# Regrouping PSUM reads in a two-layer attention step: ScalarE copies first, VectorE differences behind them, and a later return of one bank

## The chip, the cores and the metric

The kernel runs on one core of a Trainium2 chip. The time is the device time of one execution in microseconds (us); of several runs the median is given. A core has five engines that run beside each other, each through its own instructions in order: TensorE (PE, matrix products into PSUM; its weight loads are shown apart as PEld), VectorE (DVE), ScalarE (ACT), GpSimd (POOL) and SyncE (SP, which here issues DMAs). PSUM has eight banks of 128 partitions by 512 fp32 numbers; SBUF holds everything else.

## The reference

One inference step of a trunk of two layers, for 512 latent tokens and 128 context tokens, with 1024 channels, 16 heads of 64, and a feed-forward width of 2816. All is fp32. Each layer is attention and then a gated convolutional feed-forward network (FFN), each between two RMS norms with a shift, scale and gate from a conditioning vector. Cut to what matters here:

```python
for l in range(2):
    hp, hs = modulated norms of the context xp and the latents xs
    if l == 0:                       # neighbourhood attention (NA)
        q, k, v = h @ na_w_qkv
        op  = blocked_attention(qp, kp, vp)
        os_ = neighbourhood_attention(qs, ks, vs, cache_k, cache_v, na_rpb)
    else:                            # grouped-query attention (GQA), 4 heads of keys
        q, k, v = h @ gqa_w_qkv      # q and k with an RMS norm per head, rotary positions on latents
        op  = blocked_attention(qp, kp, vp)
        os_ = softmax(qs k_all^T / 8) v_all      # 512 latent + 128 cached keys
    x = x + gate * rmsnorm(o @ w_o)
    x = x + gate * rmsnorm(conv_ffn(modulated norm of x))
```

The outputs are the two streams and the new keys and values of the context.

## The kernel before, in words

**Number format.** A product of two fp32 matrices is done as three products of parts: `hi` (the number rounded by a copy into a narrower matmul format, mostly on ScalarE) and `lo` (the number less `hi`, on VectorE or GpSimd): hi·hi, hi·lo, lo·hi. So each operand that comes out of a matmul is read twice from its PSUM bank, once by the copy and once by the difference, and the bank is free for TensorE's next use only after both. Weights are split in SBUF: `wh` from `wr` at L176 on ScalarE, `wl` at L178 on VectorE or GpSimd.

**What sets the order.** All TensorE instructions are chained in the order of the program (`pe()`). A scheduler orders the other engines; `behind(a, b)` (a dependency that only sets an order) puts `a` after `b` on their engine. `Banks` is a first-in first-out queue of PSUM banks: `get` takes the one returned longest ago, `put` returns one when the last read of it has been written down in the program, not when it has run. The taker then waits on the chip for those reads.

**Stages, with the profile's times.** NA with the projections of its queries, keys and values woven in, one item of work after another (`stream()`), up to about 300 us; its output projection (`m0`) to 330; the first FFN to 810; the GQA projections to 907; the GQA attention loop to 1037; its output projection (`m1`) to 1100; the second FFN to the end.

**Queries and keys in NA.** For each pair of heads (8 pairs) the projected queries sit in one bank `qk` one after the other in two halves of the columns: one piece of 256 columns, then one of 384 with a second piece of 64 (the shapes 64x256, 64x384 and 64x64 in the profile). Each of the two heads of a pair owns 64 partitions. For each piece and head, ScalarE writes the scaled query into `qs` (L957) and VectorE the low part (L958), in turn. For keys, `k_put` writes `kh` (L925, and for all pairs but the first a second copy into the other 64 partitions, L926) and `kl` (L927).

**End of NA.** The output projection needs the attention outputs as `oh`, `ol` (L1097) and four groups of weights; `OW` says at which part of the last projection item three of those are split. The group at part 7 has its difference on VectorE, the other two on GpSimd. `kp` (L973) is a copy of a key block that TensorE transposes into `tk`.

**End of the first FFN.** For a tile of tokens, `Finish` computes the norm and the next layer's modulated input `xm`, with scalars `ro` from GpSimd (L381) and the shift in L421; these feed `tr`, TensorE's transposes. At the same time the first weights of the GQA projection are split for the product `gp`.

**GQA attention.** 32 units: 8 head pairs, each with two heads and two halves of the queries. A unit has two score tiles `s`, for each of which VectorE finds the maximum (`nmg`, L1796), ScalarE the exponentials `gp` with their sum (L1799), VectorE the reciprocal (`rcg`, L1801) and GpSimd the multiplication (L1802); this is done two units ahead of the transposes. TensorE transposes a unit's `gp` in three groups of chunks (`turns(0)`, `(1)`, `(2)`, into `tp`), each copied to `pk` (ScalarE L1813 or VectorE L1815), and `values` multiplies them into `po`, a bank that collects both halves of a pair. Four banks serve the `tp`, `po` and the leftover transposes of queries `tq`. The steps of even and odd units are

```python
GORDER = ("s0 p v s1 t0".split(), "s0 l1 l2 t0 s1 t1 t2".split())
```

where `v` is `values` of the two units before, `t` are transposes of this unit, `l` of the unit before, and `p` one leftover piece of the projections. After the second half of a pair, `po` is split into `ph` (ScalarE, L1832) and `pl` (VectorE, L1833), and the context's columns of `ph`, `pl` are split from `opr` by GpSimd (L1840, L1841).

## Time and profile before

| | |
|---|---|
| median of 3 runs | 1544.62 us (1543.17 to 1544.98) |
| profiled execution, its own time | 1544.49 us |
| its span | 1542.7 us |
| granted TensorE clock, mean | 0.999 |
| busy: PE, PEld | 1510.3 us (98%), 1342.4 us (87%) |
| busy: DVE, ACT, POOL | 1013.9 us (66%), 854.0 us (55%), 701.1 us (45%) |

In rows of the trace, the first number is the start in us from the span's start, the second the length; then engine, line, operation, out<-in (names of tiles, numbers left out), the shape, and how many instructions the row groups. `[0.95 <-DVE rcg L1801]` says that the engine stood idle for 0.95 us before the row, and which instruction ended that by the profile. Where an instruction waits for several others, the one that came last is named. Ends of matmuls are modelled, so a row's end can overlap the next row's start.

### The profile page before, as it was taken

What the parts mean: (1) busy time and instruction counts of PE and PEld (TensorE: products, weight loads), DVE (VectorE), ACT (ScalarE), POOL (GpSimd) and SP (SyncE); (2) the same over time, 40 slices, a digit from 0 to 9 for tenths busy, and PEclk for the clock granted to TensorE, in tenths of its full rate; (3) what the DMA queues carried; (4) which work ended last, traced back from release to release, by engine and by line L of the source; (5) the groups of instructions that cost most, each with busy time, mean ns of one, the idle gap of its engine ahead of it and who ended that gap; (6) DMA issues with size and microseconds to landing.
All of it is one profiled execution on the core that took longest, in us unless ns stands there. A gap on an engine that the chain in (4) does not pass through costs nothing.

```text
span 1542.7 us, 26131 instructions
## 1 busy us (share of the span) xinstructions
PE 1510.3 (98%) x9710; PEld 1342.4 (87%) x9710; DVE 1013.9 (66%) x1653; ACT 854.0 (55%) x1628; POOL 701.1 (45%) x602
## 2 busy tenths in 40 slices
PE   7999999999999999999999999999999999999998
PEld 5999989779999999988887877778999999998886
DVE  5544343659776676764747777672988887885454
ACT  5665564655655555644544447762666665564343
POOL 1655554332355445533544454432335666553433
PEclk9999999999999999999999999999999999999999
DMA  9755444263675664487574420005533334459664
GB/s 350 190 153 127 125 136 105 61 212 103 195 226 188 206 204 141 138 290 263 187 223 137 123 83 28 1 20 195 169 114 108 117 110 156 128 162 302 196 219 134
DMA packets 196667, 243.99 MB, mean 158 GB/s; under 512 B 11484, under 2 KB 153020, under 8 KB 196540
## 3 DMA queue, kind: packets, MB, share of 16 engines
q1 hardware_dynamic: 186924, 235.85, 47.6%
q10 hardware_dynamic: 9616, 6.48, 2.5%
q8 instruction: 76, 1.25, 0.3%
q14 instruction: 51, 0.42, 0.1%
HBM read 214.38 MB, written 26.34 MB: 156 GB/s over the span
## 4 chain that ended last, share of the span: by engine, by line
PE 64%; DVE 7%; issue 2%; POOL 2%; ACT 1%; DMA 1%; ACTq 0%; DVEq 0%; POOLq 0%
PE acc L117 19%; PE ux L117 17%; PE uz L117 9%; PE uy L117 5%; PE gp L117 3%; PE y L117 2%; PE s L117 2%; PE po L117 2%; PE tp L120 2%; PE ada L117 1%; DVE B L250 1%; DVE nmg L1796 1%; DMA gn<-in_gqa_k_norm 1%; DMA wr<-in_ffn_w_up 1%; DVE wl L178 0%
## 5 line engine op out<-in xcount | busy, mean ns | idle before, releaser
L178 POOL TENSOR_TENSOR wl<-wr,wh 128x1024 fp32r<-128x1024 f32 x70 | 171.2, 2450 | 238.5 <-ACT wh L176 238.3
L117 PE MATMUL ux<-B,wh 128*128 128x322 f32 x832 | 200.5, 312 | 0.7 <-ACT u L1349 0.4
L1294 POOL TENSOR_TENSOR wl<-wr,wh 128x1024 fp32r<-128x1024 f32 x76 | 181.5, 2410 | 42.1 <-ACT wh L1293 38.3
L1373 DVE SCALAR_TENSOR_TENSOR t<-C,cw,t 128x644 f32<-128x644 f32 x176 | 156.3, 888 | 51.2 <-ACT t L1370 50.7
L117 PE MATMUL acc<-wh,alo 128*128 128x512 f32 x440 | 172.0, 391 | 0.0
L117 PE MATMUL acc<-wh,ahi 128*128 128x512 f32 x440 | 171.9, 391 | 0.0
L117 PE MATMUL acc<-wl,ahi 128*128 128x512 f32 x440 | 171.8, 390 | 0.0
L176 ACT CAST wh<-wr 128x1024 fp32r<-128x1024 f32 x138 | 143.5, 1047 | 37.8 <-DMA wr<-in_ffn_w_down 26.0
L117 PE MATMUL uz<-B,wh 128*128 128x322 f32 x640 | 155.9, 312 | 0.0
L117 PEld LDWEIGHTS ux<-B,wh 128*128 128x128 f32 x832 | 143.5, 189 | 4.2 <-ACT u L1349 1.4
L1262 DVE TENSOR_TENSOR alo<-ain,ahi 128x384 fp32r<-128x384 f32 (+1 forms) x88 | 70.5, 819 | 94.0 <-ACT ahi L1260 93.7
L117 PE MATMUL ux<-B,wl 128*128 128x322 f32 x416 | 129.3, 311 | 0.2 <-DVE wl L799 0.2
L117 PE MATMUL qk<-hT,wh 128*128 128x384 f32 (+1 forms) x512 | 122.4, 315 | 0.0
L117 PEld LDWEIGHTS uz<-B,wh 128*128 128x128 f32 x640 | 110.9, 189 | 2.9 <-issue 0.8
L1293 ACT CAST wh<-wr 128x1024 fp32r<-128x1024 f32 x84 | 85.0, 1049 | 47.1 <-DVE wr L1318 46.7
L1294 POOL TENSOR_TENSOR vl<-wr,vh 128x1024 fp32r<-128x1024 f32 x38 | 98.5, 2593 | 20.0 <-ACT vh L1293 19.7
L178 DVE TENSOR_TENSOR wl<-wr,wh 128x1024 fp32r<-128x1024 f32 x68 | 91.3, 1352 | 19.3 <-ACT wh L176 18.7
L1370 ACT ACTIVATE t<-C,cw 128x644 f32<-128x644 f32 x88 | 78.6, 893 | 44.0 <-DVE C L1401 31.6
L1260 ACT CAST ahi<-ain 128x384 fp32r<-128x384 f32 (+1 forms) x88 | 39.7, 460 | 108.9 <-PE acc L117 96.6
L117 PE MATMUL uz<-B,wl 128*128 128x322 f32 x320 | 99.5, 311 | 0.4 <-POOL wl L1294 0.3
L117 PEld LDWEIGHTS acc<-wh,alo 128*128 128x128 f32 x440 | 82.6, 188 | 17.8
L117 PEld LDWEIGHTS acc<-wh,ahi 128*128 128x128 f32 x440 | 82.6, 188 | 17.8
(264 smaller groups left out, 3893.6 us busy)
## 6 DMA issues: line engine op xcount, KB each, us to landing
wr<-in_ffn_w_up SPq DMA_DIRECT2D x88, 512.0 KB
wr<-in_ffn_w_down SPq DMA_DIRECT2D x88, 512.0 KB
wr<-in_ada_w SPq DMA_DIRECT2D x72, 512.0 KB
act<-act SPq DMA_DIRECT2D x44, 321.0 KB
wr<-in_na_w_qkv SPq DMA_DIRECT2D x24, 512.0 KB
mod<-modrow SPq DMA_DIRECT2D x20, 512.0 KB
ain<-act SPq DMA_DIRECT2D x44, 192.0 KB
wf<-in_ada_w SPq DMA_DIRECT2D x16, 512.0 KB
```

What stands on the lines that cost most here:

```text
L117: pe(nc.tensor.matmul(*a, **k))
L120: pe(nc.tensor.transpose(*a, **k))
L176: i = nc.scalar.copy(hi, raw)
L178: j = (low or nc.vector).tensor_sub(lo, raw, f32(hi))
L250: return nc.vector.tensor_sub(lo, src, f32(hi))
L1260: pin(nc.scalar.copy(hi[:, 0 : c1 - c0], ain[:, 0 : c1 - c0]))
L1262: i = nc.vector.tensor_sub(lo[:, 0 : c1 - c0], ain[:, 0 : c1 - c0], f32(hi[:, 0 : c1 - c0]))
L1293: nc.scalar.copy(hl[0], src)
L1294: return low.tensor_sub(hl[1], src, f32(hl[0]))
L1370: nc.scalar.activation(t, taps(0), AF.Identity, bias=cw[:, 3, n : n + 1], scale=cw[:, 1, n : n + 1])
L1373: nc.vector.scalar_tensor_tensor(t, taps(d), cw[:, w, n : n + 1], t, op0=ALU.mult, op1=ALU.add))
L1796: self.red[i] = nc.vector.tensor_reduce(nm, sv, axis=AX.XY, op=ALU.min)
```

## The change

Five edits.

1. In NA's `k_put` and query pieces, all ScalarE copies of one bank come first, then all VectorE instructions on it. The order-only dependencies that tied `oh`/`ol` of the first two pairs to those copies (`qput`, `splits`) are gone.
2. The third group of `m0`'s weights is split at part 4 of the last item instead of part 7, with its difference on VectorE as before.
3. The order-only dependency that put the first half of `xm`'s shift behind the first `wl` of the GQA projection (`fin.moved`, `lowered`) is gone.
4. In `turn_k` and `turn_q` both heads' ScalarE copies come first, then both differences (with the DMAs that spread the keys).
5. In `values`, `po`'s bank is no longer returned at once but at the end of the next odd unit (`ta["old"]`); `pl` is put behind the VectorE copy of `turns(1)` instead of behind a reduction; and GpSimd's split of the context's columns stays in program order instead of being put behind the last norm.

```diff
-OW = {0: 0, 2: 1, 7: 2}
+OW = {0: 0, 2: 1, 4: 2}
...
-            self.moved = [
+            return [
                 nc.vector.scalar_tensor_tensor(
...
-            ]
-            return self.moved[0]
+            ][0]
...
                     i = nc.scalar.copy(d["kh"][b][own, c0:c1], src[own])
-                    j = (nc.scalar.copy if p else nc.vector.tensor_copy)(d["kh"][b][oth, c0:c1], src[own])
-                    n = nc.vector.tensor_sub(d["kl"][b][own, c0:c1], src[own], f32(d["kh"][b][own, c0:c1]))
-                while splits and c0 == 0:
-                    for x, y in zip(splits.pop(), (j, n)):
-                        behind(x, y)
+                    if p:
+                        nc.scalar.copy(d["kh"][b][oth, c0:c1], src[own])
+                for b in range(2):
+                    own, oth = own_oth(b)
+                    if not p:
+                        nc.vector.tensor_copy(d["kh"][b][oth, c0:c1], src[own])
+                    nc.vector.tensor_sub(d["kl"][b][own, c0:c1], src[own], f32(d["kh"][b][own, c0:c1]))
...
                     for qc, pc in pieces:
                         for b in range(2):
                             own, oth = own_oth(b)
+                            nc.scalar.activation(d["qs"][b][own, qc], pp[own, pc], AF.Copy, scale=-0.125)
+                    for qc, pc in pieces:
+                        for b in range(2):
+                            own, oth = own_oth(b)
                             q = d["qs"][b]
-                            j = nc.scalar.activation(q[own, qc], pp[own, pc], AF.Copy, scale=-0.125)
-                            i = nc.vector.scalar_tensor_tensor(
+                            nc.vector.scalar_tensor_tensor(
...
-            i = nc.scalar.copy(hi, of0[p]), nc.vector.tensor_sub(lo, of0[p], f32(hi))
-            if p == 0:
-                for j in range(2):
-                    behind(i[j], qput[j])
-            elif p < OEARLY:
-                splits.append(i)
+            nc.scalar.copy(hi, of0[p])
+            nc.vector.tensor_sub(lo, of0[p], f32(hi))
...
-                        m0.weights(0, OW[i], None if i == 7 else nc.gpsimd)
+                        m0.weights(0, OW[i], None if i == 4 else nc.gpsimd)
...
-                        if not i:
-                            behind(fin.moved[0], lowered[0])
...
             nc.scalar.copy(kh[own, b::2, cols], tv[own])
+        for b in range(2):
+            own, oth = own_oth(b)
             nc.vector.tensor_sub(kl[own, b::2, cols], tv[own], f32(kh[own, b::2, cols]))
...
+            nc.scalar.copy(qst[hq][b][own, :, cs], tv[own])
+        for b in range(2):
+            own, oth = own_oth(b)
             q = qst[hq][b]
-            nc.scalar.copy(q[own, :, cs], tv[own])
...
-                nc.vector.tensor_copy(x, tp[:, 0:n])
+                i = nc.vector.tensor_copy(x, tp[:, 0:n])
+                while j == 1 and held[2]:
+                    behind(held[2].pop(), i)
...
-            held[0].append(nc.vector.tensor_sub(lo[:, 0:NS], ta["po"], f32(hi[:, 0:NS])))
-            bk.put(ta["po"])
+            held[2].append(nc.vector.tensor_sub(lo[:, 0:NS], ta["po"], f32(hi[:, 0:NS])))
+            ta["old"] = ta.pop("po")
...
-                i = nc.gpsimd.tensor_scalar(hi[:, c], src, 1.0, None, op0=ALU.mult)
-                nc.gpsimd.tensor_sub(lo[:, c], src, f32(hi[:, c]))
-                tc.add_manual_dep(i.ins, last_rms[0].ins.name, no_sync, reason="order")
+                tc.keep_in_program_order(nc.gpsimd.tensor_scalar(hi[:, c], src, 1.0, None, op0=ALU.mult))
+                tc.keep_in_program_order(nc.gpsimd.tensor_sub(lo[:, c], src, f32(hi[:, c])))
...
+            if u % 2 and "old" in ta:
+                bk.put(ta.pop("old"))
```

TensorE's instructions stand in the same order before and after; those of the other engines move. Three places, each first as it was and then as it is.

VectorE in the GQA loop, around `pl` of the sixth head pair (`pk_11602` is the copy of that unit's `l1`, `pk_11630` and `pk_11635` those of `t1` and `t2` of the unit behind it). Before:

```order
L1796 TENSOR_REDUCE nmg_11542<-s2_11568 128x1
L1796 TENSOR_REDUCE nmg_11585<-s2_11588 128x1
L1833 TENSOR_TENSOR pl5_10270<-po_11461,ph5_10269 128x512
L1801 RECIPROCAL rcg_11544<-sug_11543 128x1
L1815 COPY pk_11602<-tp_11597 128x512
L1801 RECIPROCAL rcg_11587<-sug_11586 128x1
L1796 TENSOR_REDUCE nmg_11585<-s2_11616 128x1
L1815 COPY pk_11630<-tp_11625 128x512
L1815 COPY pk_11635<-tp_11632 128x256
```

And in the changed kernel:

```order
L1796 TENSOR_REDUCE nmg_11542<-s2_11568 128x1
L1796 TENSOR_REDUCE nmg_11585<-s2_11588 128x1
L1801 RECIPROCAL rcg_11544<-sug_11543 128x1
L1815 COPY pk_11602<-tp_11597 128x512
L1835 TENSOR_TENSOR pl5_10270<-po_11461,ph5_10269 128x512
L1801 RECIPROCAL rcg_11587<-sug_11586 128x1
L1796 TENSOR_REDUCE nmg_11585<-s2_11616 128x1
L1815 COPY pk_11630<-tp_11625 128x512
L1815 COPY pk_11635<-tp_11632 128x256
```

`pl5` has moved behind one reciprocal and the copy of `l1`; nothing else moved here.

GpSimd at the start of the GQA attention (`gp_10184` and `gp_10278` are the first two units' exponentials, `ph0` to `pl3` the context's columns of the first four pairs). Before:

```order
L1802 TENSOR_SCALAR gp_10185<-gp_10185,rcg_10188 128x640
L1627 TENSOR_SCALAR vh_10223<-ssh_10221 128x8
L1629 TENSOR_TENSOR rh_10225<-vh_10223,mhalf_78 128x8
L1840 TENSOR_SCALAR ph0_10259<-opr_9287 128x128
L1840 TENSOR_SCALAR ph1_10261<-opr_9287 128x128
L1841 TENSOR_TENSOR pl0_10260<-opr_9287,ph0_10259 128x128
L1841 TENSOR_TENSOR pl1_10262<-opr_9287,ph1_10261 128x128
L1840 TENSOR_SCALAR ph2_10263<-opr_9287 128x128
L1840 TENSOR_SCALAR ph3_10265<-opr_9287 128x128
L1841 TENSOR_TENSOR pl2_10264<-opr_9287,ph2_10263 128x128
L1841 TENSOR_TENSOR pl3_10266<-opr_9287,ph3_10265 128x128
L1802 TENSOR_SCALAR gp_10278<-gp_10278,rcg_10281 128x640 x2
```

And in the changed kernel:

```order
L1802 TENSOR_SCALAR gp_10185<-gp_10185,rcg_10188 128x640
L1623 TENSOR_SCALAR vh_10223<-ssh_10221 128x8
L1625 TENSOR_TENSOR rh_10225<-vh_10223,mhalf_78 128x8
L1802 TENSOR_SCALAR gp_10278<-gp_10278,rcg_10281 128x640 x2
L1802 TENSOR_SCALAR gp_10337<-gp_10337,rcg_10340 128x640 x2
L1802 TENSOR_SCALAR gp_10366<-gp_10366,rcg_10369 128x640 x2
L1802 TENSOR_SCALAR gp_10419<-gp_10419,rcg_10422 128x640 x2
L1802 TENSOR_SCALAR gp_10459<-gp_10459,rcg_10462 128x640 x2
L1802 TENSOR_SCALAR gp_10512<-gp_10512,rcg_10515 128x640
L1842 TENSOR_SCALAR ph0_10259<-opr_9287 128x128
L1843 TENSOR_TENSOR pl0_10260<-opr_9287,ph0_10259 128x128
L1802 TENSOR_SCALAR gp_10512<-gp_10512,rcg_10515 128x640
```

The eight splits no longer stand ahead of `gp_10278`; each pair's two stand between the two multiplications of a later unit.

VectorE at the end of the first FFN (`xm_9154` is the modulated input of a token tile, `wl_9201` to `wl_9237` the low parts of the first GQA weights). Before:

```order
L402 SCALAR_TENSOR_TENSOR xo_9123<-xm_9154,ro_9162,xo_9123 128x512 x2
L414 TENSOR_TENSOR xm_9154<-xo_9123,mod_8461 128x512 x2
L178 TENSOR_TENSOR wl_9201<-wr_9197,wh_9199 128x1024
L421 SCALAR_TENSOR_TENSOR xm_9154<-xm_9154,ro_9179,mod_8463 128x512 x2
L178 TENSOR_TENSOR wl_9213<-wr_9209,wh_9211 128x1024
L178 TENSOR_TENSOR wl_9225<-wr_9221,wh_9223 128x1024
L178 TENSOR_TENSOR wl_9237<-wr_9233,wh_9235 128x1024
```

And in the changed kernel:

```order
L401 SCALAR_TENSOR_TENSOR xo_9123<-xm_9154,ro_9162,xo_9123 128x512 x2
L413 TENSOR_TENSOR xm_9154<-xo_9123,mod_8461 128x512 x2
L420 SCALAR_TENSOR_TENSOR xm_9154<-xm_9154,ro_9179,mod_8463 128x512 x2
L178 TENSOR_TENSOR wl_9201<-wr_9197,wh_9199 128x1024
L178 TENSOR_TENSOR wl_9213<-wr_9209,wh_9211 128x1024
L178 TENSOR_TENSOR wl_9225<-wr_9221,wh_9223 128x1024
L178 TENSOR_TENSOR wl_9237<-wr_9233,wh_9235 128x1024
```

`xm_9154`'s shift has moved ahead of `wl_9201`; the four `wl` now stand in one run behind it.

More of the change, by code (lines that the diff above doesn't have):

```diff
@@ L164, in x_in @@
         return A["x_sample"][0, t * P : (t + 1) * P, :] if t < 4 else A["x_prompt"][0]
-    queue, lowered = [], []
+    queue = []
     def wsplit(src, a, b, low=None, own=None, pin=False, after=None, high=None, low_after=None):
@@ L183, in wsplit @@
             behind(j, after[1])
-        lowered[:] = [j]
         if low_after and not low:
@@ L483, in hybrid_step @@
     mask = tpool.tile([P, 2, 32, 8], F32, name="mask")
-    kput, plast, qput, splits = [], [], [], []
+    kput, plast = [], []
     wqkv = A["na_w_qkv"][0]
@@ L961, in part @@
                             )
-                    qput[:] = j, i
                 else:
@@ L1764, in gqa_prompt @@
         return [one, two, three]
-    sps, sps_p, ta, un, held = ExitStack(), [], {}, {}, ([], [])
+    sps, sps_p, ta, un, held = ExitStack(), [], {}, {}, ([], [], [])
     class Unit:
```

## The prediction

> **What bounds the kernel now.** I read the busy time of each engine by stage first, then the list of waits of TensorE in the stages that the change touches, then the rows around each wait. The first view gives, for a stretch of the run, the stretch's length, then the busy time of PE, PEld, DVE, ACT and POOL.
>
> ```profile
> 50.00:275.00 225.00, 223.67 (x1732) 204.27 (x1731) 99.91 (x296) 130.53 (x353) 117.39 (x119) 1.00 0.51 132
> 275.00:300.00 25.00, 22.17 (x127) 16.91 (x126) 15.91 (x40) 18.54 (x51) 9.08 (x11) 1.00 0.27 88
> 905.00:922.00 17.00, 14.90 (x134) 11.14 (x133) 12.69 (x25) 9.12 (x22) 10.60 (x17) 1.00 0.38 138
> 922.00:1038.00 116.00, 109.04 (x850) 88.27 (x849) 84.59 (x178) 81.35 (x191) 51.22 (x68) 1.00 0.04 15
> ```
>
> TensorE sets the pace: an edit elsewhere only pays where PE is idle beside it. The neighbourhood-attention loop (50 to 275) leaves 225.00 − 223.67 = 1.33 us, its end 2.83, the start of GQA attention 2.10, and the GQA loop 6.96. Those four numbers cap what this change can win. The next view lists PE's waits by what ended them (us in total, times, longest); the first two rows cover 905 to 1040, the last two 40 to 275.
>
> ```profile
> PE tp L120 <- DVE rcg L1801: 6.8, 7, 1.1
> PE tp L120 <- POOL gp L1802: 1.4, 2, 0.9
> ...
> PE po L117 <- DVE qs L958: 0.7, 3, 0.2
> PE tp L120 <- DVE qs L958: 0.4, 1, 0.4
> ```
>
> So nearly all of the idle time of the GQA loop is one wait, met seven times, once in each head pair but the last. The rows of the sixth show what it is. A pair is two halves, each closed by the 20 `po` matmuls; PE's rows first, then VectorE's.
>
> ```profile
> 1011.13 2.38 PE L117 MATMUL po<-pk,gvt 128*64 128x256 f32 x20
> 1016.94 0.63 PE L120 MATMUL tp<-ident,gp 128*128 128x128 f32 x4 [0.95 <-DVE rcg L1801]
> 1019.32 2.38 PE L117 MATMUL po<-pk,gvt 128*64 128x256 f32 x20
> 1026.58 2.38 PE L117 MATMUL po<-pk,gvt 128*64 128x256 f32 x20
> ...
> 1016.11 0.68 DVE L1833 TENSOR_TENSOR pl<-po,ph 128x512 fp32r<-128x512 f32 x1
> 1016.71 0.15 DVE L1801 RECIPROCAL rcg<-sug 128x1 f32<-128x1 f32 x1
> 1016.78 0.67 DVE L1815 COPY pk<-tp 128x512 f32<-128x512 f32 x1
> 1018.19 0.82 DVE L1796 TENSOR_REDUCE nmg<-s 128x1 f32<-128x640 f32 x1 [0.67 <-PE s L117]
> ```
>
> The view blames the reciprocal `rcg`, but that one belongs to a unit whose transposes come later. In the code the stalled transposes take the bank that `po` has just given back, and VectorE reads `po` out of it in `pl`, 1016.11 to 1016.79; `rcg` merely ends beside it. The half with the stall lasts 1019.32 − 1011.13 = 8.19 us, the next one, with the same matmuls and `po` still holding its bank, 1026.58 − 1019.32 = 7.26. **The stall is worth 0.93 us a pair.**
>
> **The change part by part.**
>
> *`po` keeps its bank to the end of the odd unit.* The stalled transposes then get the bank of an earlier transpose, whose copy ScalarE made long before, and `pl` stands behind the copy of `l1` on VectorE. What is late next? The clean half shows PE with three banks, and where VectorE stands in it:
>
> ```profile
> 1024.45 0.69 DVE L1815 COPY pk<-tp 128x512 f32<-128x512 f32 x1
> 1025.20 0.64 PEld L120 LDWEIGHTS tp<-ident,gp 128*128 128x128 f32 x6 [0.22 <-DVE pk L1815]
> 1025.28 0.82 DVE L1796 TENSOR_REDUCE nmg<-s 128x1 f32<-128x640 f32 x1
> 1026.09 1.00 DVE L1815 COPY pk<-tp 128x512 f32<-128x512 f32 x2
> ```
>
> Counted from the half's first `po`, the clean half has the `l1` copy's end at +5.82, `nmg` at +5.96 and the last copies from +6.77 on. With `pl` (0.68) and one more reciprocal (0.15) between, `nmg` starts at about +6.65 and the `t1` copy ends at about +8.1. The next `po` group starts at +7.26 and reads `t1` from its third chunk of five, two fifths of 2.31 into it (1021.63, where the next scores began, less 1019.32), so at +8.2: a tie that may cost 0.1 or so. I take 0.88 of the 0.93 for each pair: **7 × 0.88 = 6.2 us gained**; the ends are 6.5 (no tie) and 2.9 (second rival).
>
> At this place a rule speaks against the edit. The Trainium skill, "Perfetto Trace Analysis", section "Matmuls", says that independent matmul groups should rotate through different PSUM banks, so that one is emptied while the next fills; and here a bank is kept out longer. By the rule the half would get longer; by the clean half's row three banks cost PE 0.22 us, already in the 7.26.
>
> *The context columns of `ph`, `pl` on GpSimd.* They leave the block ahead of the attention and go, two instructions a pair, between two `gp` multiplications.
>
> ```profile
> 914.44 1.04 POOL L1840 TENSOR_SCALAR ph<-opr 128x128 fp32r<-128x128 f32 x2
> 917.48 0.86 POOL L1841 TENSOR_TENSOR pl<-opr,ph 128x128 fp32r<-128x128 f32 x2
> 918.33 3.13 POOL L1802 TENSOR_SCALAR gp<-gp,rcg 128x640 f32<-128x640 f32 x4
> 919.18 0.33 PE L120 MATMUL tp<-ident,gp 128*128 128x128 f32 x1 [0.91 <-POOL gp L1802]
> 919.96 0.55 PE L120 MATMUL tp<-ident,gp 128*128 128x128 f32 x3 [0.45 <-POOL gp L1802]
> ```
>
> Eight instructions, 914.44 to 918.34, stand in front of the first two `gp` that PE waits for. Without them `gp` starts some 3.9 us earlier, with the wait over before PE gets there: 0.91 + 0.45 = **1.4 us gained** (0.9 if something else holds the first; 1.9 if the lost pipelining between the two rows counts as well). In the loop the pair costs GpSimd about 0.52 + 0.43 = 0.95 us, hidden: it is busy 51.22 of 116 us there, and what it delays is transposed two units, half a pair, later. Uncovered it would cost 0.95 a pair. The order-only edits of `turn_q` in the same loop I put at nothing: ScalarE has 35 us free there.
>
> *Keys and queries of the neighbourhood loop: all ScalarE copies of a bank, then VectorE.* Now the two engines take turns on one bank:
>
> ```profile
> 155.97 0.47 ACT L957 ACTIVATE qs<-qk 64x384 fp32r<-64x384 f32 x1
> 157.28 0.57 ACT L1049 ACTIVATE p<-s,nm 128x384 f32<-128x384 f32 x1
> 157.97 0.49 ACT L957 ACTIVATE qs<-qk 64x384 fp32r<-64x384 f32 x1
> 158.82 0.56 DVE L958 SCALAR_TENSOR_TENSOR qs<-qk,qs 64x384 fp32r<-64x384 f32 x1
> 159.41 0.22 ACT L957 ACTIVATE qs<-qk 64x64 fp32r<-64x64 f32 x1 [0.95 <-DVE qs L958]
> ```
>
> The last 64-column copy waits 0.95 us for VectorE, and PE's next user of the bank waits in turn: the two lists' rows give 0.7 in three waits and 0.4 in one. I take the three as gone: **0.7 gained**, between 0 and the loop's whole 1.33. The Trainium skill, "PSUM — Partial Sum Buffer", section "PSUM bank collisions raise a hardware error", has two engines collide only in the same bank and quadrant of 32 partitions, so that copies of the other 64 partitions need not wait. The row at 159.41 differs: that copy reads the first 64 partitions and waits for a VectorE read of the other 64, so this program guards the whole bank. By the rule the term would be nil and the sum 0.7 less.
>
> *End of that stage: the third `m0` weights three parts earlier, `oh`/`ol` free of the query copies.*
>
> ```profile
> 279.05 0.33 PE L120 MATMUL tk<-ident,kp 128*128 128x128 f32 x1 [0.78 <-ACT kp L973]
> 282.39 1.04 ACT L176 CAST wh<-wr 128x1024 fp32r<-128x1024 f32 x1
> 285.93 0.50 PE L117 MATMUL y<-wh,ol 128*128 128x512 f32 x1 [1.09 <-DVE ol L1097]
> 291.81 0.66 PE L120 MATMUL tp<-ident,pp 128*128 128x128 f32 x4 [0.74 <-POOL pp L771]
> ```
>
> The cast at 282.39 now stands ahead of `kp`, whose wait of 0.78 can grow by up to 1.04; I say 0.8, since the shorter turn-taking before it gives a little back. In exchange ScalarE's and VectorE's copies for `ol` come sooner, and the wait of 1.09 goes; a short one on `kl` of about 0.2 (2.83 less these three) goes with it, and the 0.74 I leave. Together **0.5 gained**; ends 1.3 gained (0.74 gone too) and 1.0 lost (nothing gone).
>
> *End of FFN0: the order between `wl` and the shift of `xm` is dropped.* VectorE now has `xm` first, which waits for GpSimd, and the first `wl` behind it.
>
> ```profile
> 810.37 1.22 DVE L178 TENSOR_TENSOR wl<-wr,wh 128x1024 fp32r<-128x1024 f32 x1
> 812.31 1.41 DVE L421 SCALAR_TENSOR_TENSOR xm<-xm,ro,mod 128x512 f32<-128x512 f32 x2 [0.72 <-POOL ro L381]
> 813.64 3.49 DVE L178 TENSOR_TENSOR wl<-wr,wh 128x1024 fp32r<-128x1024 f32 x3
> 815.13 1.65 PE L117 MATMUL gp<-wl,hT 128*128 128x512 f32 x6
> 817.18 0.73 PE L117 MATMUL gp<-wl,hT 128*128 128x512 f32 x2 [0.40 <-DVE wl L178]
> ```
>
> `xm` cannot move up, since `ro` ends it; so all four `wl` run behind it and the last ends 1.22 later. PE already waits for the last one: the 0.40 becomes 1.6, **1.2 us lost**, and 0.2 at best if later waits in the projections soak it up. On SyncE's queue the small load of `ax` goes ahead of one weight load for a later tile; in the windows above the DMA engines are far from full, and I cost that at nothing.
>
> **Sum.** −6.2 − 1.4 − 0.7 − 0.5 + 1.2 = −7.6. The profiled execution took 1544.49 us (span 1542.7), 0.13 under the median of the three runs, so 1544.49 − 7.6 = **1536.9 us**. With the good ends, 6.5 + 1.9 + 1.3 + 1.3 − 0.2 = 10.8: 1533.7.
>
> **Rivals.** *VectorE becomes the bound of the loop.* Then each stalled half shrinks only by what `nmg` moves: +7.06 (1018.19 less 1011.13) against +6.65, 0.41, so 7 × 0.41 = 2.9, a sum of −4.3 and 1540.2. For it: VectorE's row is tightest there. Against: it is busy 84.59 of 116 us, and the clean half shows no wait of PE for scores.
>
> *Three banks starve the transposes* (the page on rotation above). The clean half's 0.22 grows by `pl`'s 0.68 if `pl` slips in ahead of the copy that frees the bank: 0.93 − 0.68 = 0.25 a pair, 1.8 in all, −3.2 and 1541.3. Against: the new order has `pl` behind that copy.
>
> *The view is right, and the wait is the reciprocal's.* Then moving the bank does nothing in the loop: −1.4 − 0.7 − 0.5 + 1.2 = −1.4 and 1543.1. Against: the same transposes run without any wait in every half where `po` keeps its bank. That the bank comes back too early after all has the same price.
>
> *Slower: the bunched copies hold up the neighbourhood loop's exponentials.* The `p` of 157.28 stood between two copies; behind four in a row (0.47 + 0.49 + 0.22 + 0.22 = 1.4 us) it, the transposes and the values of that pair come later. At the full 1.4 for 8 pairs that is 11.2 lost against 6.9 gained elsewhere: +4.3 and 1548.8; it ends slower by over 0.2% from (6.9 + 3.1) / 8 = 1.25 a pair. Against: the loop's idle of 1.33 in 225 us says that PE's other work covers most such delays.
>
> **How the numbers follow.** Forecast 0.60, VectorE as the bound 0.17, starved banks 0.05, the reciprocal 0.12, slower 0.06. A measurement here can tell about 0.2%, 3.1 us, from no change. Forecast, VectorE and half of the starved case are faster by more: 0.80; the other half and the reciprocal, with a small rest, are the same: 0.14; slower 0.06. The range goes from the good ends, 1533.7, over the first two rivals to 1542.5, leaving out the reciprocal's case and the slow one.
>
> **What would show it.** Right: the seven waits of `tp` in the GQA loop gone, halves of about 7.3 us throughout, no wait of `tp` for `gp` at the start, and a wait of `gp` for `wl` grown to about 1.6 near 817. Wrong: stalled halves still over 8 us with `pl` no longer in front of the transposes (the reciprocal), new waits for `nmg`'s followers or `pk` (the first two rivals), or new waits of PE for `p` between 50 and 275 (slower).

## The result, and the profile after

The changed kernel takes 1534.49 us (median of 6 runs, 1533.28 to 1535.53) against 1544.36 for the kernel before (6 runs, 1543.17 to 1545.6): a ratio of 0.9936, 95% interval 0.9923 to 0.9949. It is 9.9 us faster; 7.6 were forecast. The profiled execution has a span of 1533.2 us, 9.5 less than before.

First the busy times by stage, in the columns used above: stretch, length, then PE, PEld, DVE, ACT, POOL.

```profile
50.00:275.00 225.00, 225.00 (x1744) 205.84 (x1743) 100.98 (x299) 131.12 (x355) 118.22 (x120) 1.00 0.50 133
275.00:300.00 25.00, 22.83 (x132) 18.06 (x131) 16.06 (x42) 19.10 (x55) 9.76 (x12) 1.00 0.27 88
905.00:922.00 17.00, 16.13 (x160) 12.62 (x157) 13.23 (x27) 10.44 (x26) 8.20 (x11) 1.00 0.24 87
922.00:1038.00 116.00, 115.38 (x861) 93.47 (x861) 84.69 (x173) 79.50 (x187) 52.86 (x73) 1.00 0.12 39
```

The neighbourhood loop now leaves PE no idle time (1.33 us before), the GQA stretch 0.62 (6.96 before). The stretches are fixed in time and the changed kernel runs 4 to 11 us ahead in the last two, so at their edges they hold a little other work than before. In the list of PE's waits from 905 to 1040 the seven waits for `rcg` and both for `gp` on GpSimd are gone; two rows are left.

```profile
PE s L117 <- ACT gp L1799: 0.9, 1, 0.9
PE y L117 <- DVE wl L178: 0.2, 1, 0.2
```

The sixth head pair, in PE's rows (the closing `po` groups) and then around VectorE's `pl`:

```profile
1001.80 2.38 PE L117 MATMUL po<-pk,gvt 128*64 128x256 f32 x20
1009.07 2.38 PE L117 MATMUL po<-pk,gvt 128*64 128x256 f32 x20
1016.33 2.38 PE L117 MATMUL po<-pk,gvt 128*64 128x256 f32 x20
...
1006.93 0.69 DVE L1815 COPY pk<-tp 128x512 f32<-128x512 f32 x1
1007.53 0.68 DVE L1835 TENSOR_TENSOR pl<-po,ph 128x512 fp32r<-128x512 f32 x1
1007.67 0.64 PEld L120 LDWEIGHTS tp<-ident,gp 128*128 128x128 f32 x6 [0.22 <-DVE pk L1815]
```

Both halves last the same now: 7.27 and 7.26 us, where the first of them took 8.19. `pl` runs behind the copy of `l1`, and PE is already at `t1` before it ends. At the start of the attention `gp` follows its reciprocals directly, and the ten transposes run in one piece:

```profile
910.29 1.59 POOL L1802 TENSOR_SCALAR gp<-gp,rcg 128x640 f32<-128x640 f32 x2
912.96 0.56 PE L117 MATMUL s<-gkh,gq 128*128 128x320 f32 x2 [0.87 <-ACT gp L1799]
913.65 1.25 PE L120 MATMUL tp<-ident,gp 128*128 128x128 f32 x10
```

Both programs issue the same 9710 matmuls in the same order, so each matmul's start can be set against its twin's. Where the difference between the two steps, time was won or lost. Summed by place (us, minus is faster; the column "again" is a second execution of the changed kernel, the last run but one below). The sums run from the first matmul to the last. Outside them the profiled changed kernel is 0.1 earlier at the first matmul and 0.3 longer behind the last one, so its span is 9.5 less and not 9.8:

```
place                          forecast   measured   again
start of the program              0         +1.2      +0.2
neighbourhood loop              -0.7        -2.2      -2.0
its end, to 300                 -0.5        -1.4      -1.4
first FFN                         0         -0.4      -0.3
end of the first FFN            +1.2        +0.1      +0.1
GQA projections                   0         -1.0      -1.0
start of the GQA attention      -1.4        -1.8      -1.8
GQA loop                        -6.2        -5.3      -5.3
second FFN                        0         +1.0      +1.0
sum                             -7.6        -9.8     -10.5
```

### The profile page after: what moved, and what is told of

The parts are those of the page before. It is cut to its first block, busy times and chain, and to the rows that moved or that the text cites. A ratio compares the mean times of both kernels' runs of the same rounds, so it can differ in the third digit from the quotient of the medians.

```text
span 1533.2 us, 26148 instructions
## 1 busy us (share of the span) xinstructions
PE 1511.1 (99%) x9710; PEld 1344.2 (88%) x9710; DVE 1017.5 (66%) x1653; ACT 853.5 (56%) x1628; POOL 701.2 (46%) x602
## 3 DMA queue, kind: packets, MB, share of 16 engines
q8 instruction: 76, 1.25, 0.3%
## 4 chain that ended last, share of the span: by engine, by line
PE 63%; DVE 8%; issue 2%; ACT 1%; DMA 1%; POOL 1%; ACTq 0%; DVEq 0%; POOLq 0%
PE acc L117 19%; PE ux L117 17%; PE uz L117 8%; PE uy L117 4%; PE gp L117 4%; PE y L117 3%; PE po L117 2%; PE s L117 2%; PE tp L120 2%; PE ada L117 2%; DVE B L249 1%; DMA wr<-in_ffn_w_up 1%; DVE wl L178 1%; DMA gn<-in_gqa_k_norm 1%; DVE nmg L1796 1%
## 5 line engine op out<-in xcount | busy, mean ns | idle before, releaser
L1260 DVE TENSOR_TENSOR alo<-ain,ahi 128x384 fp32r<-128x384 f32 (+1 forms) x88 | 76.8, 889 | 89.0 <-ACT ahi L1258 88.5
```

What stands on the lines that cost most here:

```text
L1260: i = nc.vector.tensor_sub(lo[:, 0 : c1 - c0], ain[:, 0 : c1 - c0], f32(hi[:, 0 : c1 - c0]))
```

## The experiments

**The GQA loop: whose wait is it?** Three kernels take the two halves of that edit apart, each from the kernel before.

Bank kept, and `pl` behind the copy of `l1` (both as in the change):

```diff
-            held[0].append(nc.vector.tensor_sub(lo[:, 0:NS], ta["po"], f32(hi[:, 0:NS])))
-            bk.put(ta["po"])
+            held[2].append(nc.vector.tensor_sub(lo[:, 0:NS], ta["po"], f32(hi[:, 0:NS])))
+            ta["old"] = ta.pop("po")
...
-                nc.vector.tensor_copy(x, tp[:, 0:n])
+                i = nc.vector.tensor_copy(x, tp[:, 0:n])
+                while j == 1 and held[2]:
+                    behind(held[2].pop(), i)
...
+            if u % 2 and "old" in ta:
+                bk.put(ta.pop("old"))
```

> The kernel before, with only the bank of po kept to the end of the odd unit and pl put behind the copy of l1. Theory (the wait is for pl in po's bank): the seven waits of 0.95 us at tp go; from the matched matmuls of the two traces each is worth 1.12 us, of which 0.17 comes back as a wait of t1 for the copy of l1, and the odd pieces of the projections give back 1.2 in all: 7 x 0.95 - 1.2 = 5.4 us faster, about 1539.0. Rival (the wait is the reciprocal's, and the gain came with other edits): no change in the loop, 1544.4. Rival (the three copies and the reductions of VectorE become the bound): 2.9 faster, 1541.5.

Measured: 1539.26 us, ratio 0.9967 (0.9954 to 0.9980) against 1544.18; by matched matmuls the loop gives 5.2, against 5.3 in the changed kernel. The waits for `rcg` are gone: this edit alone makes the loop's gain.

Only the bank kept, `pl` left ahead of the copy:

```diff
-            bk.put(ta["po"])
+            ta["old"] = ta.pop("po")
...
+            if u % 2 and "old" in ta:
+                bk.put(ta.pop("old"))
```

> The kernel before, with only the bank of po kept; pl stays ahead of the copy of l1 on VectorE. Theory (bank): the transposes of t0 no longer wait, but t1 takes the bank of l1, whose copy now ends about 0.6 us later behind pl, so t1 waits about 0.8: 0.95 - 0.6 = 0.35 a pair, 2.4 us faster at most, about 1542 to 1543. Rival (reciprocal): the seven waits of 0.95 stay and nothing changes, 1544.4. Rival (the place of pl does not matter): as much as with both edits, 1539.0.

Measured: 1540.79 us, ratio 0.9977 (0.9967 to 0.9987); the loop gives 3.3, between the first and the third expectation. PE's waits from 900 to 1040:

```profile
PE tp L120 <- DVE pk L1815: 3.3, 7, 0.6
```

The seven long waits are gone though `rcg` stands where it stood, so they were the bank's. In their place stand seven at `t1` for the copy of `l1`, 0.6 to 0.7 us each by matched matmuls: `pl` in front of the copy costs that. Both halves of the edit are needed.

Only `pl` moved, the bank returned at once as before:

```diff
-            held[0].append(nc.vector.tensor_sub(lo[:, 0:NS], ta["po"], f32(hi[:, 0:NS])))
+            held[2].append(nc.vector.tensor_sub(lo[:, 0:NS], ta["po"], f32(hi[:, 0:NS])))
...
-                nc.vector.tensor_copy(x, tp[:, 0:n])
+                i = nc.vector.tensor_copy(x, tp[:, 0:n])
+                while j == 1 and held[2]:
+                    behind(held[2].pop(), i)
```

> The kernel before, with only pl moved behind the copy of l1; po's bank is given back at once as before. Theory (t0 waits for pl): pl ends about 0.8 us later, so each of the seven waits grows from 0.95 to about 1.75, 5.6 us slower, about 1550. Rival (t0 waits for the reciprocal): the reciprocal stands ahead of pl now and ends about 0.6 us earlier, so the waits shrink to about 0.4 and the kernel is 4 us faster, 1540.5.

Measured: 1549.43 us, ratio 1.0033 (1.0021 to 1.0045); the loop loses 5.2, as the first theory says. The waits, and the sixth pair's rows:

```profile
PE tp L120 <- DVE rcg L1801: 12.0, 7, 1.7
```

```profile
1018.33 0.16 DVE L1801 RECIPROCAL rcg<-sug 128x1 f32<-128x1 f32 x1
1018.40 0.69 DVE L1815 COPY pk<-tp 128x512 f32<-128x512 f32 x1
1019.01 0.68 DVE L1835 TENSOR_TENSOR pl<-po,ph 128x512 fp32r<-128x512 f32 x1
1019.61 0.15 DVE L1801 RECIPROCAL rcg<-sug 128x1 f32<-128x1 f32 x1
1019.84 0.63 PE L120 MATMUL tp<-ident,gp 128*128 128x128 f32 x4 [1.71 <-DVE rcg L1801]
```

The list still names a reciprocal, but another one: the one of 1018.33, which it named before, is done 1.4 us ahead of the transposes. What they follow in both kernels that return the bank at once is the end of `pl`: 1016.79 before and 1019.69 here, and each time they start 0.15 us behind it. The name in the list is the instruction that happened to end last ahead of the start.

**The start of the attention.** Only GpSimd's split of the context's columns moved:

```diff
-                i = nc.gpsimd.tensor_scalar(hi[:, c], src, 1.0, None, op0=ALU.mult)
-                nc.gpsimd.tensor_sub(lo[:, c], src, f32(hi[:, c]))
-                tc.add_manual_dep(i.ins, last_rms[0].ins.name, no_sync, reason="order")
+                tc.keep_in_program_order(nc.gpsimd.tensor_scalar(hi[:, c], src, 1.0, None, op0=ALU.mult))
+                tc.keep_in_program_order(nc.gpsimd.tensor_sub(lo[:, c], src, f32(hi[:, c])))
```

> The kernel before, with only GpSimd's split of the context's columns moved from the start of the attention into the loop. Theory: the block of eight instructions held gp back; the two waits of tp for gp (0.91 and 0.45) go, and matmul by matmul that is 1.8 us, nothing is lost in the loop: about 1542.6. Rival (gp was late because ScalarE and VectorE took turns on tq's bank): the waits stay, 1544.4. Rival (the inserted pair delays gp in the loop): new waits of tp for gp, up to 0.95 a pair, slower by up to 5.

Measured: 1543.29 us, ratio 0.9994 (0.9985 to 1.0004): the times alone cannot tell it from no change. The trace can: PE's list for 900 to 1040 has the seven waits of the loop and no wait for `gp` on GpSimd.

```profile
PE tp L120 <- DVE rcg L1801: 6.8, 7, 1.1
PE s L117 <- ACT gp L1799: 0.7, 1, 0.7
```

The two steps at the start are −1.07 and −0.67 us in this kernel and, to the same hundredths, in the changed one, and no step of the loop differs from before. The 1.8 is this edit's.

**The neighbourhood attention.** Only the regrouping there, of queries (shown) and keys in `k_put`, with `oh`/`ol` untied and the weights at part 7 as before:

```diff
                     for qc, pc in pieces:
                         for b in range(2):
                             own, oth = own_oth(b)
+                            nc.scalar.activation(d["qs"][b][own, qc], pp[own, pc], AF.Copy, scale=-0.125)
+                    for qc, pc in pieces:
+                        for b in range(2):
+                            own, oth = own_oth(b)
                             q = d["qs"][b]
-                            j = nc.scalar.activation(q[own, qc], pp[own, pc], AF.Copy, scale=-0.125)
-                            i = nc.vector.scalar_tensor_tensor(
+                            nc.vector.scalar_tensor_tensor(
```

> The kernel before, with only the regrouping of keys and queries in the neighbourhood attention and oh/ol of the first pairs untied from them; the weights stay at part 7. Theory (the turn-taking on one bank held TensorE's next user): the five small waits of the loop go, 2.1 us by matched matmuls against the 0.7 predicted, and at the end of the stage the waits for kl and ol go (about 0.4 and 0.9) while tk's stays at 0.8: 3 us faster in all, 1541.5. Rival (the gain of 2.1 was TensorE catching up a late start of that one execution): no step in the loop. Rival (bunched copies hold up the exponentials): new waits of tp for p between 60 and 270.

Measured: 1541.22 us, ratio 0.9980 (0.9971 to 0.9989) against 1543.97. The loop's steps are −0.36, −0.59, −0.31, −0.30 and −0.29, the same five as in the changed kernel, with smaller ones 2.2 in all; the end of the stage gives 1.6. The rival, a late start caught up, falls: this execution began 1.4 us late and the second one of the changed kernel 0.2 early, and that one still gains 2.0 here. One profiled execution gains only 0.6, that of the kernel with another order of returns (further down, the same code in this stage): it loses 1.05 in two steps near 89 and 91 us, just behind a ScalarE that had stood idle for 3.06 us. No other execution shows these steps, and why ScalarE stood there is open. In the changed kernel the place quoted in the prediction reads:

```profile
155.62 1.43 ACT L956 ACTIVATE qs<-qk 64x384 fp32r<-64x384 f32 x4
157.07 0.58 ACT L1051 ACTIVATE p<-s,nm 128x384 f32<-128x384 f32 x1
157.12 1.59 DVE L961 SCALAR_TENSOR_TENSOR qs<-qk,qs 64x384 fp32r<-64x384 f32 x4
157.65 1.04 ACT L176 CAST wh<-wr 128x1024 fp32r<-128x1024 f32 x1
159.86 2.81 PE L117 MATMUL po<-pk,vt 128*64 128x512 f32 x20
```

Four copies run back to back, then four differences. The bank is free at 158.71 instead of 160.39, and `po` does not wait. The exponential `p` starts at 157.07 against 157.28 before. The changed kernel is 0.4 us ahead at this place, so against TensorE `p` is 0.2 later, and no matmul of the loop waits for it. The four copies ahead of it did not cost it their 1.4 us, because the cast of a weight that stood between the first copy and `p` now stands behind `p`. It was, before:

```profile
156.34 1.04 ACT L176 CAST wh<-wr 128x1024 fp32r<-128x1024 f32 x1
```

**The weights at part 7 again**, the changed kernel otherwise:

```diff
-OW = {0: 0, 2: 1, 4: 2}
+OW = {0: 0, 2: 1, 7: 2}
...
-                        m0.weights(0, OW[i], None if i == 4 else nc.gpsimd)
+                        m0.weights(0, OW[i], None if i == 7 else nc.gpsimd)
```

> The changed kernel with the third group of m0's weights split at part 7 again. Theory (the cast ahead of kp made the wait of tk): tk's wait falls from 1.7 to about 0.8, and since the cast then stands between the copies for ol, about as much comes back as a wait of y for ol: within 0.5 of the changed kernel, 1534 to 1535. Rival (the bunched copies of the keys made tk late): tk keeps its 1.7. Rival (the earlier cast was a mere loss): 0.9 faster than the changed kernel, 1533.6.

Measured: 1534.46 us, ratio 0.9934 (0.9919 to 0.9949), as the changed kernel. PE's waits at that place, in the changed kernel:

```profile
278.93 0.33 PE L120 MATMUL tk<-ident,kp 128*128 128x128 f32 x1 [1.72 <-ACT kp L975]
289.23 0.63 PE L120 MATMUL tp<-ident,pp 128*128 128x128 f32 x4 [0.45 <-ACT p L1051]
```

And with the weights at part 7:

```profile
277.06 0.33 PE L120 MATMUL tk<-ident,kp 128*128 128x128 f32 x1 [0.77 <-ACT kp L975]
282.86 0.50 PE L117 MATMUL y<-wh,ol 128*128 128x512 f32 x1 [0.24 <-DVE ol L1100]
```

By matched matmuls 0.95 is won at `tk` and 0.84 lost behind it by 300. The earlier cast moves a wait and is worth about nothing; the stage's gain is the regrouping's.

**The end of the first FFN.** The dropped order put back into the changed kernel:

```diff
...
                         after(i)
+                        if not i:
+                            behind(fin.moved[0], lowered[0])
```

> The changed kernel with xm's shift behind the first wl again at the end of the first FFN. Theory (VectorE's wl slows GpSimd's small operation beside it): GpSimd's v row there goes back from 0.35 to about 1.4 us, ro and with it xm end about 1 us later, wl's last instruction ends within 0.2 of where it does now, and TensorE gains or loses nothing over 0.15 us against the changed kernel. Rival (as predicted): the four wl end 1.2 us earlier against TensorE, the wait of gp for wl goes, 0.4 to 1.2 faster.

Measured: 1535.22 us (2 runs, ratio 0.9938, 0.9918 to 0.9958). Against the changed kernel the matched matmuls move by 0.1 there. The changed kernel's rows:

```profile
807.37 0.35 POOL L373 TENSOR_SCALAR v<-sso,v 128x1 f32<-128x1 f32 x1 [0.34 <-ACT junk L371]
807.81 0.55 POOL L380 TENSOR_TENSOR ro<-v,mhalf 128x1 f32<-128x1 f32 x1
808.40 1.42 DVE L420 SCALAR_TENSOR_TENSOR xm<-xm,ro,mod 128x512 f32<-128x512 f32 x2 [0.81 <-POOL ro L380]
809.73 4.63 DVE L178 TENSOR_TENSOR wl<-wr,wh 128x1024 fp32r<-128x1024 f32 x4
814.41 0.73 PE L117 MATMUL gp<-wl,hT 128*128 128x512 f32 x2 [0.41 <-DVE wl L178]
```

With the order back:

```profile
807.75 1.40 POOL L374 TENSOR_SCALAR v<-sso,v 128x1 f32<-128x1 f32 x1 [0.33 <-ACT junk L372]
807.89 1.22 DVE L178 TENSOR_TENSOR wl<-wr,wh 128x1024 fp32r<-128x1024 f32 x1
```

GpSimd's `v`, on 128 numbers, takes 0.35 us alone and 1.40 beside VectorE's `wl`, which starts 0.14 behind it and ends 0.04 before it. So `wl` ahead of `xm` was never free: it delayed the scalar for which `xm` waits by 1.05 us.

**`turn_k` and `turn_q` in turn again**, the changed kernel otherwise:

```diff
             nc.scalar.copy(kh[own, b::2, cols], tv[own])
-        for b in range(2):
-            own, oth = own_oth(b)
             nc.vector.tensor_sub(kl[own, b::2, cols], tv[own], f32(kh[own, b::2, cols]))
...
-            nc.scalar.copy(qst[hq][b][own, :, cs], tv[own])
-        for b in range(2):
-            own, oth = own_oth(b)
             q = qst[hq][b]
+            nc.scalar.copy(q[own, :, cs], tv[own])
```

> The changed kernel with turn_k and turn_q copying and subtracting in turn again. Theory (the edit hides behind TensorE): no place moves by over 0.3 us against the changed kernel; the waits of tk in the projections, which two other runs lost as well with this code unchanged, do not come back by it. Rival (the edit shortened those waits): two waits of tk of 0.5 to 0.6 at the k tiles come back, 1.0 slower.

Measured: 1534.30 us (2 runs, ratio 0.9932, 0.9912 to 0.9952). No wait of `tk` in the projections comes back (by matched matmuls another 0.5 is gone there), and in the GQA loop two steps of 0.2 to 0.3 and smaller ones leave 0.1: this edit hides behind PE. The second FFN's step of +1.0 is missing in this run; see below.

**Can the loop give more?** First the leftover pieces behind `values`, the changed kernel otherwise:

```diff
-GORDER = ("s0 p v s1 t0".split(), "s0 l1 l2 t0 s1 t1 t2".split())
+GORDER = ("s0 v p s1 t0".split(), "s0 l1 l2 t0 s1 t1 t2".split())
```

> The changed kernel with the leftover pieces of the projections behind the values of the same even unit instead of ahead of them. Theory (their banks wait for the copy of t1, which pl has made late): the steps of 0.15 to 0.35 us beside the leftover pieces go, 1.2 us faster than the changed kernel, about 1533.3. Rival (values then start before t1 is copied): the values wait up to 0.3 in those halves and nothing is won, 1534.5. Rival (the leftover reductions now stand ahead of the reductions of the scores on VectorE): new waits of s, slower than the changed kernel by 1 to 3.

Measured: 1535.60 us, ratio 0.9941 (0.9925 to 0.9958). By matched matmuls the loop is 2.2 us slower than in the changed kernel; the times show only half of it, and the second FFN's step of +1.0 is missing here too. None of the three mechanisms did it: the `tq` pieces now hold a bank that the transposes need at once, until both `gq` differences are done.

```profile
933.49 1.17 ACT L1676 CAST gq<-tq 64x512 fp32r<-64x512 f32 x2 [0.22 <-PE tq L120]
934.93 1.39 DVE L1680 TENSOR_TENSOR gq<-tq,gq 64x512 fp32r<-64x512 f32 x2
936.47 0.85 PE L120 MATMUL tp<-ident,gp 128*128 128x128 f32 x6 [0.97 <-DVE gq L1680]
```

Then another order of returns, the changed kernel otherwise: the bank of `l2`, which ScalarE copies early, ahead of that of `l1`, and `po`'s bank right behind `t0`.

```diff
-            bk.put(tp)
+            if j == 1 and self.b == 0:
+                ta["l1"] = tp
+            else:
+                bk.put(tp)
+            if j == 2 and self.b == 0:
+                bk.put(ta.pop("l1"))
...
                     un[u].turns(int(step[1]))
+                    if u % 2 and step == "t0" and "old" in ta:
+                        bk.put(ta.pop("old"))
...
-            if u % 2 and "old" in ta:
-                bk.put(ta.pop("old"))
```

> The changed kernel with another order of returns in the GQA loop: the bank of l2 (copied by ScalarE) is returned ahead of the bank of l1 (copied by VectorE), so that t1 gets the early one, and po's bank is returned right behind t0 of the odd unit, ahead of the banks of t1 and t2. Theory (what is left of the loop's waits is which bank comes first): t1's wait of 0.17 a half goes in 16 halves, 2.7 us, and the 1.2 beside the leftover pieces go too: 3 to 4 us faster than the changed kernel, about 1531. Rival (VectorE's chain is the bound of the loop now): halves stay at 7.26, no change, 1534.5. Rival (t2 now waits for the copy of l1 as long as t1 did): only the 1.2 goes, 1533.3.

Measured: 1539.87 us, ratio 0.9965 (0.9952 to 0.9979), while the changed kernel beside it had 0.9934. By matched matmuls the loop is 2.6 us better, a little less than the 3 to 4 expected. But the scheduler's order of the second FFN's instructions on VectorE, ScalarE and SyncE came out differently behind it, and PE loses 7.5 us there against the changed kernel. Its two longest waits:

```profile
PE acc L117 <- DVE act L1382: 4.7, 1, 4.7
PE tr L120 <- DVE C L1419: 2.1, 1, 2.1
```

The changed kernel as it is, run beside these:

> The changed kernel as it is, beside the other two on one chip. All theories: 1534.5, 0.9936 of the kernel before; its profile shows which of the steps outside the edited places (the start, two waits of tk in the projections, one wait of acc in the second FFN) belong to one execution only.

Measured: 1533.96 us, ratio 0.9934 (0.9921 to 0.9946); its steps stand in the table above.

Last, the first half of that edit alone, which leaves all orders behind the loop as they are in the changed kernel:

```diff
-            bk.put(tp)
+            if j == 1 and self.b == 0:
+                ta["l1"] = tp
+            else:
+                bk.put(tp)
+            if j == 2 and self.b == 0:
+                bk.put(ta.pop("l1"))
```

> The changed kernel with the bank of l2 returned ahead of that of l1, and po's bank left at the end of the odd unit; the orders of VectorE, ScalarE and SyncE behind the loop are those of the changed kernel (in the run before this one they were not, and the second FFN lost about 7 us). Theory: each half without a leftover piece lasts 7.09 us instead of 7.26, 16 x 0.17 = 2.7 us at most, less what the leftover pieces still wait: 2 to 2.7 us faster than the changed kernel, about 1532. Rival (the loss of 7 us in the second FFN comes from the earlier end of the loop and not from the orders): 1537 to 1540. Rival (the banks of the leftover pieces get later copies): their steps grow from 0.3 to 0.6, 1 us faster, 1533.

Measured: 1534.09 us (1532.20 to 1534.19), ratio 0.9930 (0.9916 to 0.9943) against 1544.89. PE's closing groups:

```profile
999.43 2.38 PE L117 MATMUL po<-pk,gvt 128*64 128x256 f32 x20
1006.52 2.38 PE L117 MATMUL po<-pk,gvt 128*64 128x256 f32 x20
1013.62 2.38 PE L117 MATMUL po<-pk,gvt 128*64 128x256 f32 x20
```

The halves last 7.09 and 7.10 us instead of 7.27, and the loop is 1.6 better by matched matmuls, less than the 2 expected, since the leftover pieces still wait. The times do not separate it from the changed kernel: its interval holds 0.9936.

## Why the prediction was right, point by point

**The sum.** The forecast was 1536.9 us with a range from 1533.7 to 1542.5; 1534.49 lies in it, 2.4 below the forecast and 0.8 from the good end. The largest term has the right cause and nearly the right size. The rest of the sum is partly luck: three smaller terms gave 0.4 to 1.5 us more than forecast and one forecast loss of 1.2 did not come, and against them stand 0.9 missing in the loop and an unforeseen step of +1.0 in the second FFN. Without that step the sum would have come to about 1533.5, just outside the range.

**GQA loop, 6.2 forecast, 5.3 measured.** The mechanism was right: the wait was for `pl` in `po`'s bank, not for the reciprocal, and the three experiments leave no other reading. The half did shrink from 8.19 to 7.27, and 7 × 0.92 would be 6.4. What the sum missed is about 1.2 us, in two places. The four stalled halves that hold a leftover piece of the projections shrink by 0.15 to 0.34 less, 0.9 in all: there a leftover piece, or the values behind it, most likely takes the bank of `t1`, whose copy on VectorE is later than before. And the loop's last group of values, which has no scores of later units ahead of it, waits inside the group for the copy of `t1`:

```profile
1023.01 2.69 PE L117 MATMUL po<-pk,gvt 128*64 128x256 f32 x20
```

The group took 2.44 us before. VectorE's copies of `t1` and `t2` run beside it, from 1023.46 to 1024.47, and by matched matmuls it loses 0.3. The tie that the prediction saw at this copy cost nothing in the other halves and 0.3 here. "Three banks starve the transposes" was thus a small part of the truth, at other places.

**VectorE as the bound** did not come: the halves go down to 7.09 when the banks allow.

**Start of the attention, 1.4 forecast, 1.8 measured.** Shown by its own experiment. The upper end of the range was nearer: the idle time in the rows leaves out the pipelining that a broken group of transposes loses. In the rows one transpose alone takes 0.33 us, three in a row 0.55 and ten 1.25, so each further one adds only about 0.1.

**Neighbourhood loop, 0.7 forecast, 2.2 measured**, above the bound of 1.33 that the prediction took from PE's idle time. The term was mis-sized, twice. Only three of the five waits were counted; and waits shown as 0.20, 0.43 and 0.23 are steps of 0.36, 0.59 and about 0.30. So idle time in PE's rows is no upper bound for what a wait costs. The likely reason is the one above, that a matmul which starts late also loses its overlap with the one before it; this was not tested by itself. The exponentials behind bunched copies, the slower rival, made no matmul wait.

**End of the stage, 0.5 forecast, 1.4 measured.** The wait for `kp` grew by 0.94 (0.8 forecast), the waits for `ol`, `kl` and `pp` gave more than was taken for them. The earlier weights, which the prediction treated as part of this gain, contribute nothing: with them at part 7, the growth of the wait for `kp` is gone, and so is 0.84 of the gain behind it.

**End of the first FFN, 1.2 lost by forecast, 0.1 measured.** This step failed: the wait of `gp` for `wl`, forecast to grow to 1.6, is 0.41 after 0.40 before. "`xm` cannot move up, since `ro` ends it" took `ro`'s time as given, but `ro` waits for `v`, and `v` was slow only because `wl` ran beside it. Before:

```profile
810.24 1.40 POOL L374 TENSOR_SCALAR v<-sso,v 128x1 f32<-128x1 f32 x1 [0.34 <-ACT junk L372]
811.72 0.55 POOL L381 TENSOR_TENSOR ro<-v,mhalf 128x1 f32<-128x1 f32 x1
```

Taking `wl` away gave back 1.05 of its 1.22 us. The Trainium skill, "SBUF — State Buffer", section "Who interferes with whom", says that a VectorE instruction with two SBUF inputs contends with a GpSimd instruction that reads SBUF, over a port pair that they share; the 1.40 and 0.35 agree.

**What no edit made.** The projections' −1.0 is no effect of the change: five kernels with that code unchanged show −0.7 to −1.3 there too, so it was the profiled execution of before that waited at `tk` (0.51 and 0.64). The first 40 us differ by up to 2.3 us between executions with the same code there. The 0.3 to 0.4 in the first FFN, one wait of `ux` for `wl`, comes with the neighbourhood edit (0.1 of it with that edit alone, none in the four kernels that lack it) and is not explained further.

**The second FFN's +1.0** was not forecast and is only half explained. In the changed kernel VectorE's `alo` starts 0.14 us behind GpSimd's `wl` and takes 2.76 us, and the matmuls `acc` wait later:

```profile
1374.28 2.49 POOL L178 TENSOR_TENSOR wl<-wr,wh 128x1024 fp32r<-128x1024 f32 x1 [6.55 <-ACT wh L176]
1374.42 2.76 DVE L1260 TENSOR_TENSOR alo<-ain,ahi 128x384 fp32r<-128x384 f32 x1
...
1383.72 0.47 PE L117 MATMUL acc<-wh,ahi 128*128 128x512 f32 x1 [0.59 <-DVE act L1382]
```

Before, it started 0.21 ahead of GpSimd and took 0.55:

```profile
1384.89 0.55 DVE L1262 TENSOR_TENSOR alo<-ain,ahi 128x384 fp32r<-128x384 f32 x1
1385.10 2.60 POOL L178 TENSOR_TENSOR wl<-wr,wh 128x1024 fp32r<-128x1024 f32 x1 [6.56 <-ACT wh L176]
```

The same two instructions, in the other order by a third of a microsecond. The step is there in both executions of the changed kernel and in three of its variants, each time with GpSimd's `wl` first and an `alo` of 2.76 us. It is missing with `turn_k` and `turn_q` in turn, with the leftover pieces behind `values`, and in all five kernels made from the one before; in all of these `alo` is first and takes 0.55. The kernel with another order of returns has other instructions at this place and does not bear on it. What tips the order stays open.

## What to carry to other kernels

When a wait's named releaser makes no sense in the program, look at who else touches the memory that the waiting instruction writes: here a bank returned to a queue when its last read was written down, not when it had run, and the next taker paid 1.1 us. Hand a buffer back where its last reader is surely done, and try letting early-freed ones come first (1.6 us in the trace here, too little for the times to show). And before costing a moved instruction, look at what it ran beside: with VectorE's subtraction of 1.2 us out of the way, GpSimd's scalar took 1.05 us less.

## What the runs showed of the hardware

A GpSimd operation on 128 numbers took 0.35 us alone and 1.40 beside a VectorE subtraction of two SBUF operands; a VectorE subtraction took 0.55 us when it started 0.21 us ahead of GpSimd's and 2.76 when it started 0.14 behind. In the second pair the one that started later was held up; in the first, GpSimd's started 0.13 to 0.14 us earlier and was held up all the same, so which of two is held up does not follow from the starts alone. A wait that PE's rows show as 0.20 to 0.43 us cost 0.30 to 0.59, by the starts of the matmuls that follow. Ten transposes in one row took 1.25 us, one alone 0.33.
